# Packing four column blocks of the conditioning matrix on the 128 partitions, with their schedule moved, in a two-layer hybrid decoder

## The chip, the cores and the metric

One core of a Trainium2 chip runs the whole program in one launch. The metric is the device time in microseconds (us) of one execution, the median of several runs. The core has a matrix engine (PE, with its weight loads PEld), a vector engine (DVE), a scalar engine (ACT), a general engine (POOL) and a synchronising engine (SP) that here only issues DMAs.

## The reference

A sequence of 1024 tokens with 1024 features goes through two layers. Each layer first turns a conditioning vector c into six vectors of 1024 numbers:

```python
c_act = jax.nn.silu(c)
for l in range(DEPTH):
    mod = (c_act @ ada_w[l] + ada_b[l])[:, None, :]
    sh1, sc1, g1, sh2, sc2, g2 = jnp.split(mod, N_MOD, axis=-1)
    h = rms_norm(x, norm1_w[l]) * (1.0 + sc1) + sh1
    x = x + g1 * hybrid_mixer(h, w_in[l], w_out[l], ...)
    h = rms_norm(x, norm2_w[l]) * (1.0 + sc2) + sh2
    x = x + g2 * conv_ffn(h, w_gate[l], w_val[l], conv_w[l], conv_b[l], w_down[l])
return rms_norm(x, final_norm_w)
```

`ada_w[l]` is 1024 x 6144 in float32, 25.2 MB a layer. The mixer has four retention heads and four HGRN2 heads over one input projection, and one output projection. The MLP is gated, of width 2816, with a causal convolution of three taps on the gate. Everything is float32.

## The kernel before, in words

Activations lie with features on the partitions. Products run as three passes of split operands (high part, low part). A layer goes through these stages: the first units of the input projection; the heads (L862 to L882) and their gates (L885 to L897), whose projections are pairs of column blocks made of seven products (`pair`, L456); the output projection `wo` (L923 to L941); the first units of the gated MLP and its 20 pairs (L969 to L995); the down projection over three groups of feature tiles, 8, 8 and 6 (L1018 to L1038, and L1066 to L1075 for the last group, `dn_last`).

The conditioning work is called ada. `ada_w[l]` is cut into 12 blocks b of 512 columns; block b gives entries 4b to 4b+3 of the tile `mod` (128 features each). For one block, `ada_steps` (L159) takes eight loads of 128 rows x 512 columns into the tile `aw` (two buffers, SP's queue) and multiplies and adds each into the accumulator `ac` (one buffer) with the activated c of its rows as a per-partition factor: one DVE operation a load, at L165 for the first and L167 for the others. `ADA_WAIT` = 4 empty steps later, `ada_finish` (L147) sums the accumulator over the partitions with four float32 matmuls against a column of ones (L150, two passes each, into the PSUM tile `aps`), adds `ada_b` (L152), and for the scales makes `modA` (L156).

`ada_steps` is a generator: every call of `tick` (L177) goes one step further in the block that is being worked on, and a block takes 13 calls. Ticks stand in `step` (L384), which the units and pairs call after each product, and after each half in the first two groups of the down projection (L1034). Blocks 4 to 11 of layer 0 are put on the list in the first head (L877), the 12 blocks of layer 1 ahead of layer 0's MLP (L948), behind `ada_all` (L946), which runs what is left. Blocks 0 to 3 of layer 0 are made at the start by `ada_first` (L192) with loads of 512 KB, in the order 2, 0 (scale and shift of the first four feature tiles), then 3, 1.

The order of the instructions of an engine is set when the program is built, by a list scheduler that works with priorities: the place in the program text, less an offset under `hp()` (L59). The weight loads (`load_raw`, L333, two buffers on SP's queue), the splits of weights into two parts (`piece`, L326) and the additions of a product to the residual (`resid`, L908) have that offset; ada has not. An engine and its DMA queue then work in that order. Products use four PSUM banks (`pr`), transposes, sums and `aps` four others (`at`).

```python
def tick():
    if not ada_now and ada_todo:
        ada_now.append(ada_steps(*ada_todo.pop(0)))
    if ada_now and next(ada_now[0], True):
        ada_now.pop()
```

Of the kernel before, what the change touches and what calls it, by code (L numbers as in the profile page):

```python
# [9 lines left out]
F32 = mybir.dt.float32  # L10
# [4 lines left out]
ALU = mybir.AluOpType  # L15

P = 128
# [23 lines left out]
def kernel(  # L41
# [60 lines left out]

# [1 line left out]
    vec_c0 = [("c", c_in.rearrange("b (r p) -> (b r) p", p=P), 8)]  # L104
    vec_a = [("n1", norm1_w.rearrange("l (r p) -> (l r) p", p=P), 16),
# [27 lines left out]

    load_cols(0, vec_c0, nc.sync)

    def cl(name, i, n=1):
        t, r0 = col[name]
        return t[:, r0 + i:r0 + i + n]

    cact = const.tile([P, KT], F32, name="cact")  # L140
    A.activation(cact, cl("c", 0, 8), AF.Silu)

# [1 line left out]
    mod = const.tile([P, DEPTH * 48], F32, name="mod")  # L144
    modA = const.tile([P, DEPTH * 16], F32, name="modA")

    def ada_finish(l, b, a):  # L147
        ps = at_ps(f"aps{l}_{b}")
        for j in range(4):
            T.matmul(ps[:, j:j + 1], a[:, j * P:(j + 1) * P], onec, start=True, stop=True)  # L150
        o = l * 48 + b * 4
        V.tensor_tensor(out=mod[:, o:o + 4], in0=ps[:, 0:4], in1=cl("ab", o, 4), op=ALU.add)  # L152
        if b in (2, 3, 8, 9):
            which, i = (0, b - 2) if b < 4 else (1, b - 8)
            e = l * 16 + which * 8 + i * 4
            V.scalar_tensor_tensor(out=modA[:, e:e + 4], in0=mod[:, o:o + 4], scalar=1.0,  # L156
                                   in1=cl("n2" if which else "n1", l * 8 + i * 4, 4), op0=ALU.add, op1=ALU.mult)

    def ada_steps(l, b):  # L159
        a = stg.tile([P, HALF], F32, tag="ac", bufs=1, name=f"ac{l}_{b}")  # L160
        for k in range(KT):
            raw = stg.tile([P, HALF], F32, tag="aw", bufs=2, name=f"aw{l}_{b}_{k}")
            nc.sync.dma_start(out=raw, in_=ada_w[l, k * P:(k + 1) * P, b * HALF:(b + 1) * HALF])
            if k == 0:
                V.tensor_scalar_mul(a, raw, cact[:, 0:1])  # L165
            else:
                V.scalar_tensor_tensor(out=a, in0=raw, scalar=cact[:, k:k + 1], in1=a,  # L167
                                       op0=ALU.mult, op1=ALU.add)
            yield
        for _ in range(ADA_WAIT):  # L170
            yield
        ada_finish(l, b, a)

# [18 lines left out]
    def ada_first(b):  # L192
        acc = Z()
        a = acc.t[:, 0:HALF]
        for kp in range(4):
            raw = boot_pool.tile([P, S], F32, tag="boot", name=f"af{b}_{kp}")
            rv = raw[:, :].rearrange("p (a n) -> p a n", a=2)
            last_load[0] = nc.sync.dma_start(
                out=rv,
                in_=ada_w[0, kp * 256:(kp + 1) * 256, b * HALF:(b + 1) * HALF].rearrange("(a p) n -> p a n", p=P))  # L200
            for j in range(2):
                k = kp * 2 + j
                if k == 0:
                    V.tensor_scalar_mul(a, rv[:, 0, :], cact[:, 0:1])
                else:
                    V.scalar_tensor_tensor(out=a, in0=rv[:, j, :], scalar=cact[:, k:k + 1], in1=a,
                                           op0=ALU.mult, op1=ALU.add)
        ada_finish(0, b, a)
        acc.free()
# [4 lines left out]

# [1 line left out]

# [107 lines left out]

# [1 line left out]
    def piece(src, n, nm):  # L326
# [43 lines left out]

    chains = []

    def room(n):
# [10 lines left out]
    def step():  # L384
        tick()
        for ch in list(chains):
            ch[0] -= 1
            if ch[0] <= 0:
                ch[0] = next(ch[1], 0)
                if ch[0] == 0:  # L390
                    chains.remove(ch)
# [18 lines left out]

# [1 line left out]
    def split(dst, k, src):  # L412
# [120 lines left out]

# [1 line left out]
    def transpose8(src, nm, evac):  # L535
# [222 lines left out]

# [1 line left out]
    xs = [Z() for _ in range(KT)]  # L760
# [11 lines left out]
    first.keep()  # L772
    ada_first(2)
    ada_first(0)
# [3 lines left out]
    def start_units():  # L778
# [14 lines left out]
        spill_x(1, hi, nc.gpsimd)  # L793
        ada_first(3)
        ada_first(1)
# [50 lines left out]
    for l in range(DEPTH):  # L846
# [1 line left out]
        early = []  # L848
# [13 lines left out]
        for h in range(HEADS):  # L862
# [13 lines left out]
            if l == 0 and h == 0:  # L876
                ada_todo.extend((0, b) for b in range(4, 12))  # L877
            run(value_chain(a, box, "h", f"h{l}_{h}v"))
# [38 lines left out]
        def wo_cols(n):  # L917
            w = wcols(w_out, l, n * P, f"wo{l}_{n}")
            return [w[i] for i in order]

        xs = []
        load_xs(0, xd[2 * l])
        for n in range(5):  # L923
            load_xs(n + 1, xd[2 * l])
            w = wo_cols(n)
            for half in range(2):
                ps = pr_ps(f"wo{l}_{n}_{half}")
                slot_mm(ps, w, places, half)
                resid(ps, n, half, 16, xd[2 * l + 1])
        tail = {n: wo_cols(n) for n in range(5, KT)}  # L930
# [4 lines left out]
        for half in range(2):  # L935
            for n in range(5, KT):
                ps = pr_ps(f"wo{l}_{n}_{half}")
                slot_mm(ps, tail[n], places, half, hooks.get(n) if half else None)
                resid(ps, n, half, 16, xd[2 * l + 1])
            if half == 0:  # L940
                first.sums()  # L941
        second = TokenNorm(1, l, 1)
        second.sums()

# [1 line left out]
        ada_all()  # L946
        if l + 1 < DEPTH:
            ada_todo.extend((l + 1, b) for b in range(12))  # L948

        def conv_act(g, v, ft, order=None):  # L950
# [16 lines left out]
            tmp.free()  # L967

        parts = [(w_gate, l, 0, f"f{l}_0g"), (w_val, l, 0, f"f{l}_0v")]  # L969
        gps, vps = first_units([wcols(*p) for p in parts], [p[3] for p in parts], second)  # L970
# [25 lines left out]

# [1 line left out]
        places = (sum([slots(b) for b in (b11, tops[2], b21, tops[3])], []), sum([slots(b) for b in (b12, b22, b11, b21)], []),  # L998
# [19 lines left out]
        for gi, n in enumerate(GROUPS[:-1]):  # L1018
# [9 lines left out]
            for d in range(KT):  # L1028
                if gi == 0 and d + 1 < KT:
                    load_xs(d + 1, xd[2 * l + 1])  # L1030
                pss = [pr_ps(f"dn{l}_{gi}_{d}_{half}") for half in range(2)]
                for half in range(2):
                    slot_mm(pss[half], w, groups[gi], half)
                    tick()  # L1034
                w = dw(d + 1) if d + 1 < KT else None
                for half in range(2):
                    resid(pss[half], d, half, 40)
            fill(gi + 1, fresh[gi + 1], GROUPS[gi + 1])  # L1038
        f0 = starts[-1]
        nm = f"dn{l}_last"  # L1040
# [100 lines left out]
```

## Time and profile before

| | us |
|---|---|
| median of three runs (2641.31 to 2644.66) | 2642.14 |
| span of the profiled execution | 2637.6 |
| PE busy in it | 2519.4 |
| DVE busy | 1839.7 |
| ACT busy | 986.1 |
| POOL busy | 592.0 |

The time shown of the profiled execution is its span, from the first to the last instruction of the program; the runs are timed from outside it, and their median is 4.5 us above. PE's granted clock has a mean of 0.980. In the profile, `line engine op out<-in` names a group of instructions by its line in the kernel and its tiles with the numbers left out: `f` are the MLP's products, `dn` the down projection's first two groups, `wo` the output projection's, `g` the gates', `h`, `v` and `r` the heads', `aw`, `ac` and `aps` the tiles of ada, `af` the loads of `ada_first`.

### The profile page before, as it was taken

Reading aid. Unit: us, or ns where it says so; the run is one execution under the profiler, and the core shown is the slowest. Engines: PE = TensorE matmul, PEld = TensorE weight load, DVE = VectorE, ACT = ScalarE, POOL = GpSimd, SP = SyncE. Lnnn points to the kernel's source line nnn. Section 1 sums busy time; section 2 is a strip of 40 time slices with the busy share of each in tenths; the row PEclk is TensorE's granted clock in tenths of the full one; section 3 lists DMA queues with packets and bytes.
Section 4 is the critical chain, followed back from the end, with each engine's and each line's share of the span. In section 5 each row is a group of like instructions: output and inputs, shape, how many; then the busy total and the mean of one; then the engine's idle time right before and its main releaser. Section 6 shows DMA issues by size and latency. Waiting matters only on the chain.

```text
span 2637.6 us, 32740 instructions
## 1 busy us (share of the span) xinstructions
PE 2519.4 (96%) x12189; PEld 2072.7 (79%) x12189; DVE 1839.7 (70%) x2781; ACT 986.1 (37%) x1685; POOL 592.0 (22%) x480
## 2 busy tenths in 40 slices
PE   5889999999999999899999899999999999999998
PEld 4777877877788888788877788888877888887887
DVE  6988788765987788834377777777387677674435
ACT  4533433333533333412264334444154333342224
POOL 1512223210423323200023222222033332320000
PEclk8999999999999999999999999999999999999999
DMA  8222322552234344732231112224212222254213
GB/s 293 69 86 86 104 77 82 174 187 80 71 121 132 126 140 151 245 125 94 86 108 56 50 39 64 73 73 160 92 56 76 84 76 88 80 198 138 96 53 107
DMA packets 293920, 283.56 MB, mean 108 GB/s; under 512 B 10793, under 2 KB 240769, under 8 KB 293761
## 3 DMA queue, kind: packets, MB, share of 16 engines
q1 hardware_dynamic: 275904, 219.42, 26.7%
q0 software_dynamic: 17408, 61.88, 6.5%
q8 instruction: 96, 1.57, 0.2%
q14 instruction: 63, 0.52, 0.1%
q10 hardware_dynamic: 449, 0.17, 0.0%
HBM read 229.00 MB, written 52.43 MB: 107 GB/s over the span
## 4 chain that ended last, share of the span: by engine, by line
PE 71%; DVE 12%; issue 10%; POOL 4%; DMA 2%; ACT 2%; POOLq 0%; SPq 0%; DVEq 0%; ACTq 0%
PE f L451 6%; PE f L453 6%; PE f L452 6%; PE dn L528 4%; PE dn L526 4%; PE dn L527 4%; PE lh L712 2%; PE wo L526 2%; PE wo L528 2%; PE wo L527 2%; PE g L451 2%; PE g L452 2%; PE g L453 2%; PE dn_last L526 2%; PE dn_last L528 2%
## 5 line engine op out<-in xcount | busy, mean ns | idle before, releaser
L451 PE MATMUL f<-hhi,whif 128*128 128x512 f32 x640 | 253.8, 397 | 1.9 <-DVE z L485 1.8
L453 PE MATMUL f<-hhi,wlof 128*128 128x512 f32 x640 | 251.4, 393 | 0.0
L452 PE MATMUL f<-hlo,whif 128*128 128x512 f32 x640 | 250.1, 391 | 0.0
L485 DVE TENSOR_TENSOR z<-z,f 128x512 f32<-128x512 f32 x238 | 161.5, 682 | 63.1 <-PE f L453 54.0
L451 PE MATMUL f<-thi,whif 128*128 128x512 f32 x480 | 190.2, 396 | 6.0 <-ACT z L491 4.0
L452 PE MATMUL f<-tlo,whif 128*128 128x512 f32 x480 | 190.0, 396 | 0.0
L453 PE MATMUL f<-thi,wlof 128*128 128x512 f32 x480 | 189.7, 395 | 0.0
L528 PE MATMUL dn<-hhi,wlodn 128*128 128x512 f32 x384 | 151.8, 395 | 9.8 <-DVE wlodn L330 9.8
L526 PE MATMUL dn<-hhi,whidn 128*128 128x512 f32 x384 | 151.6, 395 | 0.0
L527 PE MATMUL dn<-hlo,whidn 128*128 128x512 f32 x384 | 150.1, 391 | 0.0
L167 DVE SCALAR_TENSOR_TENSOR ac<-aw,cact,ac 128x512 f32<-128x512 f32 x140 | 130.7, 934 | 22.8 <-DMA aw<-in_ada_w_dram 22.0
L912 DVE SCALAR_TENSOR_TENSOR z<-dn,mod,z 128x512 f32<-128x512 f32 x64 | 48.0, 750 | 136.3 <-PE dn L528 136.1
L453 PEld LDWEIGHTS f<-hhi,wlof 128*128 128x128 f32 x640 | 120.7, 189 | 28.4
L451 PEld LDWEIGHTS f<-hhi,whif 128*128 128x128 f32 x640 | 120.5, 188 | 28.3 <-DVE z L485 2.3
L452 PEld LDWEIGHTS f<-hlo,whif 128*128 128x128 f32 x640 | 120.6, 188 | 26.9
L451 PEld LDWEIGHTS f<-thi,whif 128*128 128x128 f32 x480 | 90.6, 189 | 29.7 <-ACT z L491 4.9
L915 POOL DMA_DIRECT2D xd<-z x48 | 26.0, 541 | 390.4 <-DVE z L912 362.5
L329 ACT ACTIVATE whidn<-rawdn 128x512 fp32r<-128x512 f32 x64 | 39.5, 627 | 186.1 <-PE dn L527 173.3
L453 PEld LDWEIGHTS f<-thi,wlof 128*128 128x128 f32 x480 | 90.6, 189 | 20.9
L452 PEld LDWEIGHTS f<-tlo,whif 128*128 128x128 f32 x480 | 90.2, 188 | 20.6
L712 PEld LDWEIGHTS lh<-z,z 128*128 128x128 f32 x640 | 80.1, 199 | 24.1 <-issue 19.6
L712 PE MATMUL lh<-z,z 128*128 128x64 f32 x640 | 80.1, 280 | 17.1 <-DVE z L731 16.3
(664 smaller groups left out, 6868.7 us busy)
## 6 DMA issues: line engine op xcount, KB each, us to landing
aw<-in_ada_w_dram SPq DMA_DIRECT2D x160, 256.0 KB, 2.7
acts<-z POOLq DMA_DIRECT2D x44, 512.0 KB, 3.2
z<-acts SPq DMA_DIRECT2D x44, 512.0 KB, 4.3
z<-xd POOLq DMA_DIRECT2D x32, 512.0 KB, 5.7
rawdn<-in_w_down_dram SPq DMA_DIRECT2D x32, 512.0 KB, 3.8
xd<-z POOLq DMA_DIRECT2D x52, 256.0 KB, 2.7
rawdn_last<-in_w_down_dram SPq DMA_DIRECT2D x32, 384.0 KB, 3.4
af<-in_ada_w_dram SPq DMA_DIRECT2D x16, 512.0 KB, 9.9
```

What stands on the lines that cost most here:

```text
L167: V.scalar_tensor_tensor(out=a, in0=raw, scalar=cact[:, k:k + 1], in1=a, op0=ALU.mult, op1=ALU.add)
L329: A.activation(hi[:, 0:n], src, AF.Copy)
L451: T.matmul(ps, wh, rh, start=k == 0, stop=False)
L452: T.matmul(ps, wh, rl, start=False, stop=False)
L453: T.matmul(ps, wl, rh, start=False, stop=k == 3)
L485: V.tensor_add(o, x, ps)
L526: T.matmul(ps, a, rh, start=i == 0, stop=False)
L527: T.matmul(ps, a, rl, start=False, stop=False)
L528: T.matmul(ps, b, rh, start=False, stop=i == last)
L712: T.matmul(ps[:, c * 64:(c + 1) * 64].rearrange("p (b t) -> p b t", t=s), k.t[:, cs], qp.t[:, cs].rearrange("p (b t) -> p b t", t=s)[:, 1: ...
L912: V.scalar_tensor_tensor(out=x, in0=ps, scalar=mod[:, l * 48 + gate + d:][:, 0:1], in1=x, op0=ALU.mult, op1=ALU.add)
L915: nc.gpsimd.dma_start(out=dst[d, :, sl], in_=x)
```

## The change

A load of `ada_steps` now takes 32 rows of four neighbouring blocks: block q of the four lies on partitions 32q to 32q+31. A pack of four blocks needs 32 loads of 256 KB, 32 operations and 37 steps. Its finish makes the four matmuls against a mask `msk` of four columns (column q is one on block q's partitions), so that one pass gives the sums of all four blocks. There are two packs of layer 0 (blocks 4 and 8) and three of layer 1 (0, 4 and 8). `ada_first` packs two blocks on 64 partitions each, b and b + 2, with 16 loads of 256 KB a pack, each into one half of the partitions. The factors are laid out anew by `load_c` for two and for four blocks.

The ticks change place: none in the MLP's units and pairs of either layer (`quiet`), two behind each half of the output projection's first five column tiles and of the first half of its last three, and three in place of one behind each half of the down projection. Layer 1's packs are put on the list ahead of the output projection, and `ada_all` stands ahead of it and again behind the second group of the down projection.

```diff
+    def load_c(q):
+        n = P // q
+        zz = Z()
+        src = c_in.rearrange("b (j r) -> (b j) r", r=n)
+        for i in range(q):
+            nc.sync.dma_start(out=zz.t[0:D // n, i * n:(i + 1) * n], in_=src)
+        ps = at_ps(f"cps{q}")
+        T.transpose(ps[:, 0:D // n], zz.t[0:D // n, 0:P], ident[0:D // n, 0:D // n])
+        cact[q] = const.tile([P, D // n], F32, name=f"cact{q}")
+        A.activation(cact[q], ps[:, 0:D // n], AF.Silu)
+        zz.free()
+        msk[q] = const.tile([P, q], F32, name=f"msk{q}")
+        V.memset(msk[q], 0.0)
+        for i in range(q):
+            V.memset(msk[q][i * n:(i + 1) * n, i:i + 1], 1.0)
...
-    def ada_finish(l, b, a):
+    def ada_finish(l, b, gap, q, a):
         ps = at_ps(f"aps{l}_{b}")
         for j in range(4):
-            T.matmul(ps[:, j:j + 1], a[:, j * P:(j + 1) * P], onec, start=True, stop=True)
+            T.matmul(ps[:, j * q:(j + 1) * q], a[:, j * P:(j + 1) * P], msk[q], start=True, stop=True)
...
     def ada_steps(l, b):
         a = stg.tile([P, HALF], F32, tag="ac", bufs=1, name=f"ac{l}_{b}")
-        for k in range(KT):
+        for k in range(32):
             raw = stg.tile([P, HALF], F32, tag="aw", bufs=2, name=f"aw{l}_{b}_{k}")
-            nc.sync.dma_start(out=raw, in_=ada_w[l, k * P:(k + 1) * P, b * HALF:(b + 1) * HALF])
+            nc.sync.dma_start(out=raw, in_=ada_w[l, k * 32:(k + 1) * 32, b * HALF:(b + 4) * HALF].rearrange(
+                "r (q n) -> q r n", q=4))
...
-        ada_finish(l, b, a)
+        ada_finish(l, b, 1, 4, a)
+        if b != 4:
+            ada_scale(l, b // 8, 0, 8)
...
     def ada_first(b):
...
-        for kp in range(4):
+        for kp in range(8):
             raw = boot_pool.tile([P, S], F32, tag="boot", name=f"af{b}_{kp}")
             rv = raw[:, :].rearrange("p (a n) -> p a n", a=2)
-            last_load[0] = nc.sync.dma_start(
-                out=rv,
-                in_=ada_w[0, kp * 256:(kp + 1) * 256, b * HALF:(b + 1) * HALF].rearrange("(a p) n -> p a n", p=P))
+            for q in range(2):
+                last_load[0] = nc.sync.dma_start(
+                    out=rv[q * 64:(q + 1) * 64],
+                    in_=ada_w[0, kp * 128:(kp + 1) * 128, (b + 2 * q) * HALF:(b + 2 * q + 1) * HALF].rearrange(
+                        "(a r) n -> r a n", r=64))
...
     def step():
-        tick()
+        if not quiet[0]:
+            tick()
...
-    ada_first(2)
+    load_c(4)
     ada_first(0)
...
-        ada_first(3)
         ada_first(1)
...
-                ada_todo.extend((0, b) for b in range(4, 12))
+                ada_todo.extend((0, b) for b in (4, 8))
...
+        ada_all()
+        if l + 1 < DEPTH:
+            ada_todo.extend((l + 1, b) for b in (0, 4, 8))
         xs = []
         load_xs(0, xd[2 * l])
         for n in range(5):
...
                 slot_mm(ps, w, places, half)
+                tick()
+                tick()
                 resid(ps, n, half, 16, xd[2 * l + 1])
...
+                if not half:
+                    tick()
+                    tick()
                 resid(ps, n, half, 16, xd[2 * l + 1])
...
-        ada_all()
-        if l + 1 < DEPTH:
-            ada_todo.extend((l + 1, b) for b in range(12))
...
+        quiet[0] = True
         parts = [(w_gate, l, 0, f"f{l}_0g"), (w_val, l, 0, f"f{l}_0v")]
...
                     slot_mm(pss[half], w, groups[gi], half)
                     tick()
+                    tick()
+                    tick()
...
+        quiet[0] = False
+        ada_all()
```

## Rows read from the trace of the kernel before

**Rows 1.** The page's first line of busy times, and its chain that ended last by engine.
```profile
PE 2519.4 (96%) x12189; PEld 2072.7 (79%) x12189; DVE 1839.7 (70%) x2781; ACT 986.1 (37%) x1685; POOL 592.0 (22%) x480
...
PE 71%; DVE 12%; issue 10%; POOL 4%; DMA 2%; ACT 2%; POOLq 0%; SPq 0%; DVEq 0%; ACTq 0%
```

**Rows 2.** Windows: length, busy PE, PEld, DVE, ACT, POOL (count), clock, DMA share, GB/s.
```profile
99.70:551.50 451.80, 415.82 (x2425) 350.73 (x2424) 370.48 (x620) 173.60 (x358) 116.34 (x79) 0.97 0.34 107
...
694.60:1098.90 404.30, 399.99 (x1761) 325.43 (x1760) 335.89 (x443) 145.49 (x218) 126.91 (x103) 1.00 0.45 142
1098.90:1286.00 187.10, 179.46 (x778) 146.26 (x777) 76.54 (x101) 37.31 (x50) 2.64 (x5) 0.98 0.36 117
1407.00:1836.30 429.30, 406.81 (x2361) 343.55 (x2360) 315.82 (x534) 171.79 (x351) 104.30 (x74) 0.98 0.23 73
...
1978.00:2370.30 392.30, 388.69 (x1680) 315.60 (x1679) 280.38 (x353) 149.69 (x218) 122.28 (x106) 1.00 0.30 98
2370.30:2551.40 181.10, 178.98 (x771) 145.64 (x770) 66.99 (x86) 37.51 (x51) 1.06 (x2) 0.99 0.31 102
```

**Rows 3.** Timeline of PE around one finish: start, length, instruction.
```profile
450.40 0.95 PE L150 MATMUL aps<-onec,ac 128*128 128x1 f32 x8
451.27 1.15 PE L722 MATMUL lh<-z,z 128*64 128x64 f32 x16
```

**Rows 4.** Groups by line, whole span: busy us, mean ns, idle before and releasers.
```profile
L167 DVE SCALAR_TENSOR_TENSOR ac<-aw,cact,ac 128x512 f32<-128x512 f32 x140 | 130.7, 934 | 22.8 <-DMA aw<-in_ada_w_dram 22.0
...
L150 PE MATMUL aps<-onec,ac 128*128 128x1 f32 x160 | 18.9, 239 | 0.0
```

**Rows 5.** Timeline of DVE: finishes of three blocks, one block's first operation.
```profile
287.10 0.16 DVE L152 TENSOR_TENSOR mod<-aps,cols 128x4 f32<-128x4 f32 x1
...
454.05 0.15 DVE L152 TENSOR_TENSOR mod<-aps,cols 128x4 f32<-128x4 f32 x1
...
543.22 0.15 DVE L152 TENSOR_TENSOR mod<-aps,cols 128x4 f32<-128x4 f32 x1
543.29 0.48 DVE L165 TENSOR_SCALAR ac<-aw,cact 128x512 f32<-128x512 f32 x1
```

**Rows 6.** Tile `ac` in the heads, then in two blocks: durations, first and last start.
```profile
L167 DVE SCALAR_TENSOR_TENSOR ac<-aw,cact,ac x57: 734/746/2853, 122.3 to 543.8; 128x512 f32<-128x512 f32 x57
L165 DVE TENSOR_SCALAR ac<-aw,cact x9: 475/479/485, 121.8 to 543.3; 128x512 f32<-128x512 f32 x9
...
L167 DVE SCALAR_TENSOR_TENSOR ac<-aw,cact,ac x7: 734/743/2853, 456.9 to 474.0; 128x512 f32<-128x512 f32 x7
...
L167 DVE SCALAR_TENSOR_TENSOR ac<-aw,cact,ac x7: 740/745/752, 226.4 to 251.7; 128x512 f32<-128x512 f32 x7
```

**Rows 7.** The page's DMA queues (packets, MB, share of 16 engines) and one load.
```profile
q0 software_dynamic: 17408, 61.88, 6.5%
...
q10 hardware_dynamic: 449, 0.17, 0.0%
...
aw<-in_ada_w_dram SPq DMA_DIRECT2D x160, 256.0 KB, 2.7
```

**Rows 8.** Timeline of DVE in the down projection: start, length, instruction, idle before.
```profile
1132.97 0.75 DVE L167 SCALAR_TENSOR_TENSOR ac<-aw,cact,ac 128x512 f32<-128x512 f32 x1 [0.85 <-DMA aw<-in_ada_w_dram]
...
1143.27 0.75 DVE L167 SCALAR_TENSOR_TENSOR ac<-aw,cact,ac 128x512 f32<-128x512 f32 x1 [1.31 <-DMA aw<-in_ada_w_dram]
...
1147.51 0.75 DVE L912 SCALAR_TENSOR_TENSOR z<-dn,mod,z 128x512 f32<-128x512 f32 x1 [2.22 <-PE dn L528]
...
1153.07 0.75 DVE L912 SCALAR_TENSOR_TENSOR z<-dn,mod,z 128x512 f32<-128x512 f32 x1 [1.66 <-PE dn L528]
```

**Rows 9.** Window of the start, columns as in rows 2.
```profile
12.00:24.00 12.00, 9.24 (x46) 8.49 (x44) 7.99 (x28) 7.35 (x13) 0.00 (x0) 0.88 1.07 364
```

**Rows 10.** Line L198, the loads of `ada_first`: durations of an issue, first and last start.
```profile
L198 SPq DMA_DIRECT2D af<-in_ada_w_dram x16: 368/522/799, 7.1 to 31.2; - x16
```

**Rows 11.** Timeline of PE at the start.
```profile
30.28 1.87 PE L150 MATMUL aps<-onec,z 128*128 128x1 f32 x8 [6.75 <-DVE z L206]
```

More of the change, by code (lines that the diff above doesn't have):

```diff
@@ L100, in open_tops @@
             tops[i + 1] = (thi[:, i], tlo[:, i])
-    vec_c0 = [("c", c_in.rearrange("b (r p) -> (b r) p", p=P), 8)]
     vec_a = [("n1", norm1_w.rearrange("l (r p) -> (l r) p", p=P), 16),
@@ L132, in load_cols @@
             zz.free()
-    load_cols(0, vec_c0, nc.sync)
+    msk, cact = {}, {}
+    def load_c(q):
[13 more added lines that the diff above has]
+            V.memset(msk[q][i * n:(i + 1) * n, i:i + 1], 1.0)
+    load_c(2)
     def cl(name, i, n=1):
@@ L138, in cl @@
         return t[:, r0 + i:r0 + i + n]
-    cact = const.tile([P, KT], F32, name="cact")
-    A.activation(cact, cl("c", 0, 8), AF.Silu)
     mod = const.tile([P, DEPTH * 48], F32, name="mod")
     modA = const.tile([P, DEPTH * 16], F32, name="modA")
-    def ada_finish(l, b, a):
+    def ada_finish(l, b, gap, q, a):
         ps = at_ps(f"aps{l}_{b}")
         for j in range(4):
-            T.matmul(ps[:, j:j + 1], a[:, j * P:(j + 1) * P], onec, start=True, stop=True)
+            T.matmul(ps[:, j * q:(j + 1) * q], a[:, j * P:(j + 1) * P], msk[q], start=True, stop=True)
@@ L151, in ada_finish @@
         o = l * 48 + b * 4
[L152 to L157, printed above, removed]
+        pick = lambda t: t.rearrange("p (q m) -> p q m", q=q)[:, :, 0:4]
@@ L159, in ada_steps, with ada_scale @@
+        V.tensor_tensor(out=pick(mod[:, o:o + q * gap * 4]), in0=ps[:, 0:4 * q].rearrange("p (j q) -> p q j", q=q),
+                        in1=pick(cl("ab", o, q * gap * 4)), op=ALU.add)
+    def ada_scale(l, which, i, n):
+        e, o = l * 16 + which * 8 + i, l * 48 + which * 24 + 8 + i
+        V.scalar_tensor_tensor(out=modA[:, e:e + n], in0=mod[:, o:o + n], scalar=1.0,
+                               in1=cl("n2" if which else "n1", l * 8 + i, n), op0=ALU.add, op1=ALU.mult)
     def ada_steps(l, b):
@@ L160, in ada_steps @@
         a = stg.tile([P, HALF], F32, tag="ac", bufs=1, name=f"ac{l}_{b}")
-        for k in range(KT):
+        for k in range(32):
             raw = stg.tile([P, HALF], F32, tag="aw", bufs=2, name=f"aw{l}_{b}_{k}")
-            nc.sync.dma_start(out=raw, in_=ada_w[l, k * P:(k + 1) * P, b * HALF:(b + 1) * HALF])
+            nc.sync.dma_start(out=raw, in_=ada_w[l, k * 32:(k + 1) * 32, b * HALF:(b + 4) * HALF].rearrange(
+                "r (q n) -> q r n", q=4))
             if k == 0:
-                V.tensor_scalar_mul(a, raw, cact[:, 0:1])
+                V.tensor_scalar_mul(a, raw, cact[4][:, 0:1])
@@ L166, in ada_steps @@
             else:
-                V.scalar_tensor_tensor(out=a, in0=raw, scalar=cact[:, k:k + 1], in1=a,
+                V.scalar_tensor_tensor(out=a, in0=raw, scalar=cact[4][:, k:k + 1], in1=a,
                                        op0=ALU.mult, op1=ALU.add)
@@ L203, in ada_first @@
                 if k == 0:
-                    V.tensor_scalar_mul(a, rv[:, 0, :], cact[:, 0:1])
+                    V.tensor_scalar_mul(a, rv[:, 0, :], cact[2][:, 0:1])
                 else:
-                    V.scalar_tensor_tensor(out=a, in0=rv[:, j, :], scalar=cact[:, k:k + 1], in1=a,
+                    V.scalar_tensor_tensor(out=a, in0=rv[:, j, :], scalar=cact[2][:, k:k + 1], in1=a,
                                            op0=ALU.mult, op1=ALU.add)
-        ada_finish(0, b, a)
+        ada_finish(0, b, 2, 2, a)
+        ada_scale(0, 0, b * 4, 4)
         acc.free()
@@ L371 @@
     chains = []
+    quiet = [False]
     def room(n):
```

## The prediction

> **What bounds the kernel now.** I read the page's totals and the chain of waits first. PE is busy 96% of the span and carries 71% of the chain that ended last, with DVE next at 12% [rows 1]: time is won only where PE waits or does avoidable work, and lost wherever something makes PE wait. Then I cut the span at the first matmul of each stage and laid the stages of layer 0, which carry the modulation work (ada: loads, accumulating DVE operations, summing matmuls), beside the same stages of layer 1, which carry none [rows 2]. That gives the present price of this work. The heads and gates take 451.8 us against 429.3, the pairs of the MLP 404.3 against 392.3, the first two groups of the down projection 187.1 against 181.1. So all the work that the change touches costs about 40 us after the start.
>
> The sum is made against the profiled execution: span 2637.6 us. The median of the runs, 2642.1, is 4.5 us above that span and holds what lies around it. The prediction is for the median. A difference under 0.2% (5.3 us) is what a measurement of this kernel cannot tell from none.
>
> **What is removed.** A block's finish is eight passes of PE, one after the other: 0.87 us from its start to that of the next matmul, 450.40 to 451.27 [rows 3]. With four blocks in one pass it happens 5 times in place of 20, and twice in place of 4 at the start. Three more columns in a pass, which lasts 239 ns by the mean [rows 4], I cost at nothing. The 17 small additions that go with the finishes (0.15 us of DVE each) I leave out of the sum, as a gain of at most 2.6 us. The accumulating operations do not become fewer: a pack of four blocks has 32, as four blocks of eight had, each 934 ns by the mean [rows 4], each with a 256 KB load.
>
> - The MLP's pairs lose all of this work. The diff also stops the ticks there. They become what layer 1's are: **-12**.
> - The down projection's base becomes that of layer 1: **-6** (mostly its start, where DVE was late with the last column tile).
> - The heads lose six finishes: 6 x 0.87 = **-5**.
> - Three finishes land in the down projection: 3 x 0.87 = **+3**.
>
> **Where the work really goes.** The diff writes 26 ticks into the output projection and 96 into the down projection. The rows say that a block does not wait for its tick: the first operation of layer 1's first block ran at 543.29, right behind the finish of layer 0's last block at 543.22 [rows 5]. Its written place is in the MLP's pairs, which start at 694.6. What holds a block back is only its single accumulator, which comes free at the finish before it. The finish itself stays near its written place: a block takes 13 steps, and the third and sixth block's finishes (steps 39 and 78) stand at 287.10 and 454.05 [rows 5], 4.3 us per step. So I expect: layer 0's two packs run from about 122 and from the 37th step (about 278 us), layer 1's first pack runs from the 74th step (about 437) and so still among the gates, its finish waits until the down projection, and the other two packs, 64 operations, run in the down projection, each as fast as its loads and DVE allow.
>
> - The heads and gates then hold 96 operations in place of 66, 57 and 9 [rows 6]. The 66 with their 8 finishes cost 22.5 us over layer 1; less 8 x 0.87 that is 15.5 us, or 0.23 us each. 30 more: **+7** (0 if the surplus has another cause).
>
> **The loads.** This is the part that the trace of before does not show. A load of one block has 128 rows on both sides. The new one has 128 partitions on its target side, but its source counts 4 (column blocks) first, then 32 rows. How far a load is spread can be read off one queue: q10, the vector loads on ACT's queue, shows 449 packets and 0.17 MB [rows 7]. Those loads have 16, 16, 8, 8, 8, 8, 44, 96, 66 and 66 rows of 512 B, in all 336 rows and 0.172 MB; the other 113 packets carry next to nothing. 113 is just 16+16+8+8+8+8+11+16+11+11: one closing packet for each part, the parts being the largest number up to 16 that divides the rows. So a load's leading count sets how many DMA engines share it. With a leading count of 4 on one side, the bounds are 4 engines and 16. I take 4, because the rows follow exact divisors and 4 divides both sides, while 16 does not divide the source's 4.
>
> [...]
>
> The price goes by rows: q0, with large packets, moved 61.88 MB in 6.5% of 16 engines' span, that is 44 us per MB and engine [rows 7]. A quarter of 256 KB per engine takes 2.8 us (64 KB), a sixteenth 0.7. A load that lands in 2.7 us [rows 7] would land in about 4.8. Two buffers and 0.75 us of DVE then allow one operation per (4.8 + 0.75)/2 = 2.8 us, which is also what the four engines allow when they serve nothing else.
>
> - *Down projection.* Other traffic takes a share of 0.31 of the engines there [rows 2], so 2.8 becomes up to 2.8/(1 - 0.31) = 4.1 us; as the stage stretches by a third that share falls to about 0.23, so 3.6. The spacing now is (1143.27 - 1132.97)/5 = 2.06 us [rows 8]. DVE works in order, so a pack of 32 that was laid out at 2.06 keeps the queue back by 32 x 1.54 = 49 us, and with it the residual additions and the weight splits behind. PE bears some of that: with four PSUM banks, a half of 5.56 us (two residual additions, 1147.51 and 1153.07 [rows 8]) needs the bank of three halves earlier, a slack of 16.7 us. Loss per pack 49 - 17 = 32, for two packs 64; I take **+60**, from 2 x (32 x 0.74 - 17) = 14 (engines otherwise free) to 2 x (32 x 2.0 - 17) = 94.
> - *Heads and gates.* At a share of 0.23 [rows 2] the limit is 3.6 us. Two blocks of before were spaced (474.0 - 456.9)/6 = 2.85 and (251.7 - 226.4)/6 = 4.2 us [rows 6], mean 3.5, so DVE's own load nearly covers it. From 0 to 96 x 0.75 = 72; I take **+15**, nearer the low end since the mean spacing almost fits.
> - *Start.* The stretch from 12 to 24 us moves 364 GB/s at a full share [rows 9], and the summed loads become 32 of half the partitions, with four small loads ahead on SP's queue. Eight more issues at 0.5 us [rows 10] and four small ones delay the second half of x by up to 6 us, mostly behind the 16 operations of DVE that end at 30.28 [rows 11]; the first of its two finishes (1.9 us, beside DVE's work) goes, and the first scaled tile (0.75 us) comes behind the second. The second Silu and eight fills of small masks are taken as covered by ACT's and DVE's other work here; without that cover they cost some 2 us, which the bounds hold. **+2**, from -2 to +10.
>
> [...]
>
> SP's queue also holds the weight loads: a load of ada that waits for its buffer keeps the next weights back. That is within the lag above, since both follow DVE.
>
> **Sum:** -12 - 6 - 5 + 3 + 7 + 60 + 15 + 2 = +64 us. Span about 2701, median about **2705 us**: slower by 2.4%.
>
> **Rivals.**
> - *The loads use all 16 engines.* Then both lags vanish and the start is even: -12 - 6 - 5 + 3 + 7 = -13, about 2629 us, faster. For it: nothing in the rows shows a load with unequal sides. Against it: the exact divisors of q10. It decides at the landing: under about 3.4 us (two buffers at 2.06 us per operation) the lag is gone.
> - *Narrow loads, but an order that gives way.* If the list spreads the 64 operations evenly over the 181 us, one per 2.8 us, narrow loads just fit: -11, about 2631 us. For it: the diff's own ticks are nearly as sparse. Against it: the block that ran at once [rows 5] and the spacing of 2.06.
> - *The work stays where it is written.* Then 26 operations stand in the output projection at two per half and 70 in the down projection at three per half. At 3.6 us each a half of the latter needs 10.8 in place of 5.56: 23 halves x 5.2 - 17 = 103 us; the other terms -18, about 2727 us.
>
> **How the numbers follow.** Forecast 0.53, its own range 2650 to 2765 (the bounds of its unknown costs, not all at one end). All 16 engines 0.20, the order that gives way 0.10, the written place 0.07, and 0.10 for narrow loads with a loss that just cancels the gains, on either side of zero. Faster: 0.20 + 0.09 + 0.03 = 0.32; within 0.2%: 0.05; slower: 0.63. The range must reach to the faster rivals, since together they hold 3 in 10: from 2618 to 2770.
>
> **What would show it.** The median landing of the ada loads near 4.8 us or above in place of 2.7; the packets of SP's queue fewer although the bytes are the same; 40 summing passes in place of 160; DVE's idle time on those loads well above 22 us and mostly between 1100 and 1340; the MLP's pairs at 392 us; the first two groups of the down projection near 245 us, with PE waiting for a residual addition. A landing of 2.7 us, or a down projection near 184 us, proves the forecast wrong.

## The result and the profile after

The changed kernel takes **2862.2 us** (median of four runs, 2860.6 to 2864.5) against 2643.4 for the kernel before: a ratio of 1.083, 95% interval 1.081 to 1.084. It is slower by 219 us. The prediction named the sign and the cause, but its size, +64 us, and its range, up to 2770, were far too small.

The page of the changed kernel: busy times, SP's queue, the chain by engine, and the accumulating operations (busy us, mean ns, idle before them and what ended it).

```profile
PE 2577.5 (90%) x12054; PEld 2096.2 (73%) x12054; DVE 1828.4 (64%) x2768; ACT 989.6 (35%) x1687; POOL 569.9 (20%) x480
...
q1 hardware_dynamic: 274480, 219.44, 25.8%
...
PE 63%; DMA 15%; DVE 13%; issue 6%; POOL 2%; ACT 1%; SPq 0%; DVEq 0%; POOLq 0%; ACTq 0%
...
L185 DVE SCALAR_TENSOR_TENSOR ac<-aw,cact,ac 128x512 f32<-128x512 f32 x155 | 120.7, 779 | 248.0 <-DMA aw<-in_ada_w_dram 247.8
```

Beside [rows 1] and [rows 4]: DMA goes from 2% of the chain to 15%, and DVE's idle time before the accumulating operations from 22.8 to 248.0 us. These 225 us more are about as much as the loss of 219. That the wait is its cause, and not only its companion, the experiments below have to show.

The same page of the kernel before has for SP's queue:

```profile
q1 hardware_dynamic: 275904, 219.42, 26.7%
```

The bytes are the same and the packets 1424 fewer. That is what 4 closing packets per ada load give in place of 16: 160 x 12 = 1920 fewer, less 256 for the 16 more loads at the start and 240 for the loads of c.

Windows of the changed kernel by stage, cut at the first matmul of each; columns as in [rows 2]. In order: layer 0's heads and gates, output projection up to the MLP, MLP's pairs, first two groups of the down projection; then layer 1's heads and MLP.

```profile
104.60:666.20 561.60, 442.53 (x2377) 366.71 (x2376) 386.57 (x640) 169.24 (x352) 111.33 (x78) 0.89 0.33 97
666.20:824.30 158.10, 147.10 (x620) 116.71 (x619) 93.54 (x142) 61.64 (x97) 29.07 (x31) 0.95 0.29 89
824.30:1270.20 445.90, 409.65 (x1682) 327.72 (x1681) 298.52 (x386) 147.01 (x217) 116.94 (x106) 0.95 0.33 105
1270.20:1503.60 233.40, 191.14 (x785) 152.84 (x784) 89.48 (x121) 37.16 (x51) 1.06 (x2) 0.90 0.36 113
1624.60:2056.70 432.10, 410.19 (x2360) 345.46 (x2359) 315.91 (x534) 171.65 (x352) 104.90 (x74) 0.97 0.23 73
2197.90:2594.00 396.10, 392.49 (x1681) 315.19 (x1680) 280.67 (x352) 150.59 (x218) 119.43 (x106) 1.00 0.30 97
```

Against [rows 2] the heads and gates grew by 110 us, the stretch up to the MLP by 15, the MLP by 42, the down projection by 46, the start by 5; layer 1 hardly moved (432.1 and 396.1 us against 429.3 and 392.3). In the heads PE's busy time itself grew from 415.8 to 442.5 us with fewer instructions: the mean granted clock fell from 0.97 to 0.89 while PE waited more. So some 27 of those 110 us are matmuls run slower, not more of them.

Timeline of PE in the changed kernel, the third and the last pack's finish:

```profile
785.68 0.95 PE L165 MATMUL aps<-msk,ac 128*128 128x4 f32 x8
787.45 0.79 PE L390 MATMUL uf_0g<-hhi,whif_0g 128*128 128x512 f32 x1 [0.82 <-ACT hhi L345]
...
1459.59 0.40 PE L553 MATMUL dn<-hhi,wlodn 128*128 128x512 f32 x1
1482.32 1.87 PE L165 MATMUL aps<-msk,ac 128*128 128x4 f32 x8 [22.33 <-DVE ac L185]
```

Timeline of DVE in the changed kernel: the third pack's addition, the next pack's first operation, then two operations in the down projection.

```profile
835.18 0.16 DVE L168 TENSOR_TENSOR mod<-aps,cols 128x16 f32<-128x16 f32 x1
...
835.94 0.48 DVE L183 TENSOR_SCALAR ac<-aw,cact 128x512 f32<-128x512 f32 x1
...
1415.93 0.75 DVE L185 SCALAR_TENSOR_TENSOR ac<-aw,cact,ac 128x512 f32<-128x512 f32 x1 [2.40 <-DMA aw<-in_ada_w_dram]
1418.58 0.75 DVE L185 SCALAR_TENSOR_TENSOR ac<-aw,cact,ac 128x512 f32<-128x512 f32 x1 [1.90 <-DMA aw<-in_ada_w_dram]
```

The packs began at 127.3, 322.7, 514.3, 835.9 and 1372.0 us. The third finish stands in PE's order at 785.68, among the first products of the MLP and just ahead of a wait for ACT (787.45), so the fourth pack ran in the MLP, where the diff stops the ticks. Only the fifth ran in the down projection. There PE stood for 22.33 us in front of the last finish, whose data were late, with the projection's matmuls queued behind it.

### The profile page after: what moved, and what is told of

Read it like the earlier page. It is cut to its first block, busy times and chain, and to the rows that moved or that the text cites. A ratio compares the mean times of both kernels' runs of the same rounds, so it can differ in the third digit from the quotient of the medians.

```text
span 2861.7 us, 32494 instructions
## 1 busy us (share of the span) xinstructions
PE 2577.5 (90%) x12054; PEld 2096.2 (73%) x12054; DVE 1828.4 (64%) x2768; ACT 989.6 (35%) x1687; POOL 569.9 (20%) x480
## 4 chain that ended last, share of the span: by engine, by line
PE 63%; DMA 15%; DVE 13%; issue 6%; POOL 2%; ACT 1%; SPq 0%; DVEq 0%; POOLq 0%; ACTq 0%
DMA aw<-in_ada_w_dram 12%; PE f L476 7%; PE f L478 7%; PE f L477 7%; PE dn L553 3%; PE dn L551 3%; PE dn L552 3%; PE lh L737 2%; PE wo L551 2%; PE wo L553 2%; PE wo L552 2%; DVE ac L185 2%; PE dn_last L551 2%; PE dn_last L553 2%; PE dn_last L552 2%
## 5 line engine op out<-in xcount | busy, mean ns | idle before, releaser
L185 DVE SCALAR_TENSOR_TENSOR ac<-aw,cact,ac 128x512 f32<-128x512 f32 x155 | 120.7, 779 | 248.0 <-DMA aw<-in_ada_w_dram 247.8
```

The costliest lines, as they stand in the source:

```text
L185: V.scalar_tensor_tensor(out=a, in0=raw, scalar=cact[4][:, k:k + 1], in1=a, op0=ALU.mult, op1=ALU.add)
```

## The experiments

Theory N: the packed load's source counts 4 first, so 4 of 16 engines carry it, and DVE, which works in order, waits for it. Rival S: the place of the work costs the time.

**Wide loads in the changed kernel** (e1_wide). Rows first, then column blocks; mask and c to match.

```diff
-                "r (q n) -> q r n", q=4))
+                "r (q n) -> r q n", q=4))
```

> The changed kernel with one thing altered: its packed loads go row by row (32 rows first, then the 4 column blocks), so that partition 4r+q holds row r of block q; the cact columns and the summing mask are laid out to match. Bytes, number of loads, operations and the order on PE, ACT and DVE after the start stay. Theory N (a load whose leading count is 4 is carried by 4 of the 16 DMA engines, and DVE's queue waits for it): the loss goes, and what the packing saves stays. 2642 less 15 finishes x 0.87 plus about 5 at the start: about 2635 us, 2615 to 2650. DVE idle on the ada loads falls from 248 us to under 40; packets of SP's queue 274480 + 160 x 12 - 3 x 48 = 276256; the heads and gates of layer 0 near 450 us, the MLP's pairs near 400. Rival S (the place of the 160 operations costs the time: a pack in the MLP's pairs, one in the down projection, one accumulator): stays above 2800 us whatever carries the loads. Rival L (what counts is that a row of 2 KB comes from four far places): also above 2800.

Measured 2684.1 us, ratio 1.015 (1.013 to 1.016). SP's packets and the idle time, from its page:

```profile
q1 hardware_dynamic: 276256, 219.43, 27.5%
...
L193 DVE SCALAR_TENSOR_TENSOR ac<-aw,cact,ac 128x512 f32<-128x512 f32 x155 | 129.9, 838 | 55.5 <-DMA aw<-in_ada_w_dram 54.2
```

Windows of the heads, the MLP and the down projection:

```profile
104.80:570.80 466.00, 420.09 (x2378) 351.82 (x2377) 390.00 (x641) 171.72 (x355) 112.85 (x78) 0.95 0.38 118
...
720.10:1128.00 407.90, 395.78 (x1682) 316.20 (x1680) 302.63 (x386) 147.12 (x217) 120.33 (x106) 1.00 0.36 115
1128.00:1316.90 188.90, 184.29 (x786) 148.37 (x785) 89.30 (x121) 37.54 (x51) 1.07 (x2) 0.98 0.45 139
```

The packets are the number expected, and **178 of the 219 us go with the order of one access pattern**: by the profiles 95.6 in the heads, 38.0 in the MLP, 44.5 in the down projection, and 9 between. (These add up to 187: the profiled run of e1_wide was the fastest of its four, 2675.7 us against 2683.0 to 2685.3.) With 96, 32 and 32 operations that is 1.0, 1.2 and 1.4 us for each. S falls, and so does L, the rival that rows from four far places cost the time. But 39 us remain where the expectation had none.

**Narrow loads in the kernel before** (e2_narrow4, e2_narrow8). Only its loads are altered, and the columns of c.

```diff
-            nc.sync.dma_start(out=raw, in_=ada_w[l, k * P:(k + 1) * P, b * HALF:(b + 1) * HALF])
+            nc.sync.dma_start(out=raw, in_=ada_w[l, k * P:(k + 1) * P, b * HALF:(b + 1) * HALF].rearrange(
+                "(r q) n -> q r n", q=NQ))
```

With NQ = 4:

> The kernel before with only its 160 ada loads altered: the same 128 rows of 2 KB, taken as 4 groups of 32 (every fourth row), so that the source counts 4 first; the cact columns follow. Blocks, finishes, ticks and the order of PE and DVE stay those of before. Theory N: the loss of the change appears without the change: the changed kernel loses about 50 us per 32 operations (heads, MLP and down projection alike), so 160 lose about 220: 2860 us, 2780 to 2920; DVE idle on the ada loads from 22 us to 200 or more; packets of SP's queue 275904 - 160 x 12 + 24 = 274008. Rival S: 2642, within 10 us.

Measured 2806.5 us, ratio 1.062 (1.060 to 1.063). From its page, then windows of the heads and the MLP:

```profile
q1 hardware_dynamic: 274000, 219.42, 26.4%
...
L178 DVE SCALAR_TENSOR_TENSOR ac<-aw,cactn,ac 128x512 f32<-128x512 f32 x140 | 119.2, 851 | 199.1 <-DMA aw<-in_ada_w_dram 198.6
```

```profile
99.40:611.60 512.20, 435.09 (x2426) 363.98 (x2426) 364.21 (x619) 172.83 (x356) 112.37 (x79) 0.93 0.32 94
...
755.20:1256.20 501.00, 434.37 (x1761) 339.83 (x1760) 329.63 (x443) 144.07 (x217) 118.70 (x104) 0.94 0.39 115
```

The loss appears without the change: 161 us, 60 in the heads for 66 operations and 97 in the MLP for 88. The packets are 4 closing ones per load (the 8 under the expected count are a slip in the sum: the extra load of c has 8 rows and 8 closing packets).

With NQ = 8:

> e2_narrow4 with 8 groups of 16 rows in place of 4 of 32: the source counts 8 first. Theory N: 8 engines carry a load, 32 KB each, so one operation per 1.4 us is the floor and few spacings of the kernel before are under it: 2645 to 2680 us, DVE idle on the ada loads 30 to 80 us, packets of SP's queue 275904 - 160 x 8 + 16 = 274640. Rival R (any load whose rows are taken out of order or in groups costs the same): near 2806, as with 4 groups.

Measured 2704.7 us, ratio 1.023 (1.021 to 1.024), so 60 us more than before, beyond the expected 35. From its page:

```profile
q1 hardware_dynamic: 274640, 219.42, 27.0%
...
L178 DVE SCALAR_TENSOR_TENSOR ac<-aw,cactn,ac 128x512 f32<-128x512 f32 x140 | 124.7, 891 | 94.3 <-DMA aw<-in_ada_w_dram 93.7
```

The loss runs with the leading count: 0 with 16 closing packets a load, 60 us with 8, 161 us with 4. Rival R, that any load taken in groups costs the same, falls.

**The start of before, with wide loads** (e5_wide_oldstart). Four blocks of 128 rows each; shown is what selects them.

```diff
-    load_c(2)
+    load_c(1)
...
-        ada_finish(0, b, 2, 2, a)
+        ada_finish(0, b, 1, 1, a)
```

> e1_wide with the start of before: four blocks of 128 rows by four loads each, four finishes, in place of two packs of two by loads of 64 partitions. If the half-width loads at the start cost what the stage cut shows (r starts at 104.6 in place of 99.7 us), this is 3 to 7 us faster than e1_wide; if the start is even, within 3 us of it.

Measured 2667.5 us, ratio 1.0090 (1.0075 to 1.0105): 16.6 us faster than with the packed start by the medians, while by the profiles the window of the heads begins at 96.8 in place of 104.8, 8.0 us sooner. The pair e4_wide_oldplace and e7_wide_unpaced below differs in the start too, and there the medians are 8.7 us apart. Windows of the start, first of the changed kernel (12 to 24 us, where SP's queue moves almost only half-width loads), then of this one (12 to 18 us, where it moves only the full-width ones):

```profile
12.00:18.00 6.00, 5.26 (x30) 4.90 (x31) 3.10 (x18) 5.84 (x11) 0.00 (x0) 1.00 0.89 217
18.00:24.00 6.00, 0.88 (x9) 0.72 (x7) 5.62 (x16) 2.85 (x5) 0.00 (x0) 0.57 1.07 245
```

```profile
12.00:18.00 6.00, 3.69 (x24) 2.52 (x22) 5.54 (x21) 5.50 (x11) 0.00 (x0) 1.00 1.04 379
```

At a full DMA share (last column but one, 1.07 and 1.04) the half-width loads move 245 GB/s, the full-width ones 379.

**The place of the work** (e4_wide_oldplace, e7_wide_unpaced). Wide loads with the ticks where they were before, first with the packed start, then with the old one; the ticks between the matmuls of the output and down projections go too.

```diff
-        ada_all()
-        if l + 1 < DEPTH:
-            ada_todo.extend((l + 1, b) for b in (0, 4, 8))
         xs = []
...
-        quiet[0] = True
+        ada_all()
+        if l + 1 < DEPTH:
+            ada_todo.extend((l + 1, b) for b in (0, 4, 8))
```

> e1_wide with the ticks put back where the kernel before has them (every step of heads, gates and MLP; none added in the output and down projections), so packing without the move. Theory N: the place matters little once loads are wide; within 15 us of e1_wide, 2620 to 2650. Rival S: at least 100 us faster than e1_wide.

> Packs of four blocks with wide loads, the start of before and the ticks where the kernel before has them: e5_wide_oldstart and e4_wide_oldplace in one. 2667 less the 5 us between e1 and e4: about 2662, 2652 to 2672.

Measured 2678.7 us (ratio 1.013, 1.011 to 1.015) and 2670.0 us (1.009, 1.008 to 1.011): within 6 us of the same kernels with the moved ticks. With wide loads, moving the ticks is worth next to nothing either way. It moves little, too: only the fifth pack changes its stage, and begins at 938 in place of 1231 us in one pair and at 923 in place of 1222 in the other. What the move is worth with narrow loads no run shows.

**Pace** (e6_wide_paced, e9_wide_spread). In the kernel of e7_wide_unpaced, each accumulating operation is put behind the last addition of its own step on DVE's queue; the second kernel adds an idle step after every second operation and waits 2 steps in place of 4 ahead of the finish.

```diff
-            with nullcontext():
+            with paced():
                 if k == 0:
...
             yield
+            if k % 2:
+                yield
```

> e7_wide_unpaced with each accumulating operation of the packs put behind the last addition of its own step in DVE's queue, so that a pack spreads over its 37 steps. Theory D (what is left of the loss with wide loads, some 22 us without the start, comes of a pack's 32 operations running as densely as DVE allows once the accumulator is free): 20 to 30 us faster than e7, near 2635. Rival: the operations cost DVE the same wherever they stand, within 6 us of e7.

> e6_wide_paced with one idle step after every second operation and a shorter wait before the finish (51 steps a pack in place of 37), so that the 160 operations fill the steps of heads, gates and MLP evenly: 64 in the heads and gates over some 106 steps. Theory D (density decides): the heads cost per operation what they cost before, 0.22 us in place of 0.44 in e6; heads and gates near 447 us in place of 461, the MLP near 400, in all 2630 to 2640, faster than the kernel before by 0.2 to 0.5%. Rival: pacing has nothing left to give, 2647 as e6.

Measured 2647.3 us (ratio 1.0012, 1.0003 to 1.0022) and 2642.0 us (0.9991, 0.9982 to 1.0001). Windows of the heads and the MLP, unpaced, paced, spread:

```profile
95.40:561.40 466.00, 420.68 (x2378) 351.24 (x2377) 396.92 (x643) 173.41 (x357) 113.75 (x80) 0.96 0.39 119
710.30:1124.40 414.10, 399.52 (x1698) 317.37 (x1697) 328.16 (x421) 145.58 (x217) 126.15 (x106) 1.00 0.42 132
```

```profile
97.00:558.00 461.00, 419.01 (x2378) 349.70 (x2378) 369.94 (x616) 176.75 (x359) 115.21 (x80) 0.96 0.34 104
699.40:1100.60 401.20, 397.20 (x1705) 319.37 (x1704) 351.11 (x448) 144.65 (x217) 130.59 (x106) 1.00 0.49 154
```

```profile
97.00:551.80 454.80, 415.46 (x2377) 348.24 (x2376) 373.49 (x617) 176.66 (x359) 119.08 (x80) 0.96 0.34 106
693.20:1091.30 398.10, 394.49 (x1697) 317.56 (x1696) 333.02 (x439) 147.02 (x217) 127.98 (x106) 1.00 0.49 152
```

Pacing is worth 22.8 us. The MLP shows it best: 414 to 401 us, although it then holds 91 of the 160 accumulating operations in place of 64. A pack that may run as soon as its accumulator is free crowds DVE there, where PE needs it. In the heads the gain is not shown: 466 to 461 us, with 64 operations in place of 96. Another 7.5 us lie between the two stages (148.9 to 141.4), which hold none of these operations unpaced and 5 paced; their cause stays open. Spreading further gives 5 more and brings the heads to 454.8 with the same 64 operations, not the 447 expected. The spread kernel is level with the kernel before; it does not beat it.

**Pace with narrow loads** (e8_narrow_paced), the second rival of the prediction: the paced kernel with the loads of the changed one.

> e6_wide_paced with the loads of the changed kernel (4 column blocks first). The order that gives way, second rival of the prediction: with operations some 4.3 us apart a narrow load of 2.7 us fits between, and it is within 30 us of e6. Otherwise, if other traffic on the same 4 engines or the pairs of loads keep DVE waiting at that spacing too, it is 80 us or more slower than e6.

Measured 2770.5 us, ratio 1.048 (1.046 to 1.049). From its page:

```profile
L192 DVE SCALAR_TENSOR_TENSOR ac<-aw,cact,ac 128x512 f32<-128x512 f32 x155 | 127.7, 824 | 134.6 <-DMA aw<-in_ada_w_dram 134.1
```

It is 123 us slower than e6, and DVE's idle time on the ada loads is 134.1 us against 7.5. An order that gives way softens the narrow loads but does not make them fit.

**Which engines, and how many loads at once** (e10_two_queues, e11_pool_queue, e12_three_buffers). The changed kernel with its odd loads on ACT's queue; with all on POOL's; with three buffers.

```diff
-            nc.sync.dma_start(out=raw, in_=ada_w[l, k * 32:(k + 1) * 32, ...
+            (nc.scalar if k % 2 else nc.sync).dma_start(out=raw, in_=ada_w[l, k * 32:(k + 1) * 32, ...
```

> The changed kernel with its odd ada loads issued from ACT's queue in place of SP's. If every load whose source counts 4 is carried by the same 4 engines, two queues share them and the floor between operations in the down projection stays at 2.65 to 2.7 us; 2862, within 40 us. If one queue carries one such load after the other and a second queue brings other engines, the floor falls to about 1.35 us, and DVE idle on the ada loads from 248 to under 130 us; 2720 to 2790.

Measured 2854.9 us (ratio 1.080, 1.078 to 1.082), idle on the loads 241.0 us. From its page:

```profile
q10 hardware_dynamic: 11009, 21.15, 2.3%
...
L185 DVE SCALAR_TENSOR_TENSOR ac<-aw,cact,ac 128x512 f32<-128x512 f32 x155 | 120.9, 780 | 241.2 <-DMA aw<-in_ada_w_dram 241.0
```

ACT's queue went from 449 to 11009 packets: 80 x (128 + 4). That the time stays does not yet show that both queues share the same 4 engines, since two buffers would hold back a faster pair of queues too. The trace shows it. A window of the last pack, in which only ada loads move, on both queues (columns as before, DMA share and GB/s last):

```profile
1401.00:1406.00 5.00, 3.96 (x18) 2.87 (x16) 1.64 (x3) 0.00 (x0) 0.00 (x0) 1.00 0.25 84
```

The share stays at 4 of 16 engines. At 254 moments of the last pack, sampled every 0.05 us, packets of both queues were in flight, and 203 times they were 4 together, never more than 6.

> The changed kernel with all its packed ada loads issued from POOL's queue in place of SP's. Two queues shared the same 4 engines in e10. If POOL's queue gives each load 4 engines in turn, two loads in flight do not share engines: the floor between operations in the down projection falls from 2.65 towards 1.4 us, DVE idle on the ada loads from 248 to 60 to 150 us, 2690 to 2800 in all. If the engines are the same whatever the queue, 2862 within 40 us; if POOL's own work holds the issues back, slower than 2862 and DVE idle above 248 us.

Measured 2863.0 us (ratio 1.083, 1.080 to 1.086). From its page:

```profile
aw<-in_ada_w_dram POOLq DMA_DIRECT2D x160, 256.0 KB, 5.9
```

This is the one place where a narrow load's landing is shown: 5.9 us against 2.7 [rows 7]. The time is what was expected if the engines are the same whatever the queue, but for another reason: with two buffers, a landing of 5.9 us and 0.75 us of DVE give one operation per 3.3 us even if the engines differ. The trace shows that here they do differ at times. A window of the last pack with two loads in flight and no other transfer:

```profile
1448.00:1449.50 1.50, 1.50 (x8) 1.21 (x7) 0.00 (x0) 0.00 (x0) 0.00 (x0) 1.00 0.51 157
```

Half of the 16 engines' time is taken, and 157 GB/s are moved, where two queues of the run before kept to 0.25 and 84. On POOL's queue a load also comes to 272 packets in place of 132, so its count can't be read beside that of SP's.

> The changed kernel with three buffers for the ada loads in place of two (and, to make room, five in place of six for the low halves of the weights). If two buffers and a landing near 5.9 us set the mean of 3.53 us between operations of the last pack, a third brings it to the floor of the 4 engines, 2.65 to 2.9 us, DVE idle on the ada loads from 248 to 120 to 180 us and the time to 2740 to 2810. If the 4 engines are the limit at all times, 2862 within 20 us. If the fifth buffer of the weights matters more than either, slower.

Measured 2854.0 us (ratio 1.081, 1.079 to 1.083). Timeline of DVE in its down projection; a window of its last pack in which only ada loads move; ACT's waits for weights between 1264 and 1500 us; and the order of SP's queue beside one of those waits:

```profile
1295.63 0.75 DVE L185 SCALAR_TENSOR_TENSOR ac<-aw,cact,ac 128x512 f32<-128x512 f32 x1 [1.26 <-DMA aw<-in_ada_w_dram]
1298.31 0.75 DVE L185 SCALAR_TENSOR_TENSOR ac<-aw,cact,ac 128x512 f32<-128x512 f32 x1 [1.92 <-DMA aw<-in_ada_w_dram]
```

```profile
1406.50:1420.00 13.50, 5.98 (x18) 4.47 (x17) 4.06 (x6) 1.15 (x2) 0.00 (x0) 0.75 0.26 98
```

```profile
ACT whidn L352 <- DMA rawdn<-in_w_down_dram: 158.8, 7, 25.2
```

```profile
1302.36 0.45 SPq L363 DMA_DIRECT2D rawdn<-in_w_down_dram  x1
1304.44 24.26 SPq L180 DMA_DIRECT2D aw<-in_ada_w_dram  x9
1328.77 0.45 SPq L363 DMA_DIRECT2D rawdn<-in_w_down_dram  x1
...
1337.90 1.15 ACT L352 ACTIVATE whidn<-rawdn 128x512 fp32r<-128x512 f32 x2 [25.23 <-DMA rawdn<-in_w_down_dram]
```

A third buffer does bring the operations of these packs to the floor, 2.68 us apart for long stretches, and with three loads on their way the engines still move 98 GB/s at a share of 0.26: four of 16. It gains only 8 us by the medians (0.2% by the ratios, whose intervals overlap), and DVE's idle time on the ada loads stays at 233.8 us, well above the expectation. The third finish kept its place here, so the MLP without a pack took 394.3 us and the down projection with two 257.0; the heads took 578.1. The weights of the down projection now wait: ACT stood 158.8 us for them, against 34.7 in the changed kernel between 1270 and 1504, which had one pack there. SP's lines show why: nine ada loads stand between two weight loads on its queue, so the weight loads were issued 26.4 us apart, and ACT's wait of 25.23 us is that interval less its own 1.15. The weight load itself took 9.1 us from its issue to ACT's use, against a median landing of 3.8 in the kernel before, so it came later as well, but the 26.4 us between the issues are the larger part. (One buffer fewer for the low halves of the weights is in this run as well.)

## Why the prediction was wrong in size

**What closes the sum.** By medians: 2862.2, less 178.1 for wide loads, 16.6 for the start, 22.8 for the pace, plus 2.5 for the place, gives 2647.2; the kernel before stood at 2639 to 2646 in these comparisons. The terms follow one path through the runs (after, e1, e5, e7, e6), so they add up by construction; what they show is that nothing is left at its end. By the other way round the start is 8.7 and the place -5.4, so each small term is good to some 8 us.

**Term by term**, forecast against the profiles: heads and gates -5 + 7 + 15 = +17, measured +110; the stretch up to the MLP no term, +15; the MLP -12, +42; the down projection -6 + 3 + 60 = +57, +46; the start +2, +5; the rest none, +6. In all +64 against +224.

- **Four engines: right.** The share of 0.26 with loads always on their way (e12) and of 0.25 with two queues at work (e10) shows it, and the floor of 2.65 us (estimated 2.8) and the loss by leading count (161 us with 4, 60 with 8) go with it. The closing packets go with the source's count although the target has 128 partitions: 4 per load where the source counts 4 (e2_narrow4), 8 where it counts 8 (e2_narrow8).
- **The step that failed: heads and gates, +15, "nearer the low end since the mean spacing almost fits".** Measured: 95.6 us by e1_wide, above even the bound of 72. A mean spacing of 3.25 to 3.5 against a limit of 3.6 says nothing, since operations come in bursts. Of the 57 spacings inside blocks of the heads in the kernel before, 33 are under 3.6 us, and what they lack adds up to 64.6 us; the narrow loads cost the kernel before 60.4 us in that stage (e2_narrow4). Over all 140 spacings the same sum gives 173 us, against 161 measured. The sum leans on its limit: with 2.65 us in place of 3.6 it gives 36 and 91. Time spent in a long spacing is not paid back to a short one, because DVE works in order. The trace for this sum was at hand; I averaged it.
- **MLP, -12: wrong, +42.** The step that failed is "its finish waits until the down projection". It stands in PE's order at 785.68, which freed the accumulator some 500 us ahead of its written place, the 11th of the 96 ticks of a stage that began at 1270.2. The rule that I took from [rows 5], that a block starts when the accumulator is free, held four times out of four, within 4 us; I did not apply the same freedom to the finish.
- **Down projection, +57: measured +46, but for one pack, not two.** A pack cost 46 us where I had 30. Twenty-two of them are PE waiting at the finish, a wait that I had not seen: the finish's matmuls stand in PE's order in front of the projection's. In the run with three buffers both packs landed there, and the stage took 257.0 us against the 245 forecast. So +57 came near +46 by luck: too many packs at too low a price.
- **30 more operations in the heads, +7 less 5: too small.** With wide loads that stage still grew by 14 us. The 0.23 us were read from blocks that pause for 5 steps after every 8, and a pack does not pause. That this is the reason is not shown: spreading the same 64 operations (e6 to e9) took 6 us off the heads, but pacing, which took 32 of 96 operations out of them, only 5.
- **The stretch up to the MLP, no term: measured +15.** With wide loads it grew by 6, so 9 of the 15 go with the narrow loads.
- **Start, +2, bounds -2 to +10: the stage began 4.9 us later than before and 8.0 later than in the same kernel with the old start; by medians 16.6 (e1 to e5), beyond the bound, or 8.7 (e4 to e7), inside it.** About 8 of the 16.6 are the distance of the profiled run of e1 from its median, so they are not in its profile, and where they lie stays open. The price was near the upper bound, and I took a value near the lower one. Both bounds were my estimates: the trace of before holds no half-width load of ada. In the changed kernel such loads moved 245 GB/s (18 to 24 us), in e5 the full-width ones 379 (12 to 18 us), both at a full DMA share; why they move less is not shown.
- **The saved finishes (15 fewer at 0.87 us, -13 over layer 0): not seen in the total.** The spread kernel has 40 summing passes in place of 160, wide loads and the old start, and is level with the kernel before. In the MLP, with eight finishes fewer and 84 operations in place of 80, it took 398.1 us against 404.3; its heads took 454.8 against 451.8, with 64 operations in place of 66. What lengthens the heads was not settled.
- **The rivals.** All 16 engines: refuted by the packets (4 closing ones a load) and the share (0.25 in e10, 0.26 in e12). The order that gives way: with operations paced to their own steps, further apart than this rival asked for, narrow loads still cost 123 us. The work where it is written: not what happened, though 2727 was the nearest of my figures.
- **Two slips in the working, neither of weight:** [rows 2] give the DMA share of layer 1's down projection as 0.32, not 0.31, and 2 x (32 x 0.74 - 17) is 13.4, not 14.

## What to carry to other kernels

Before packing several column blocks into one load, write out which count comes first in its source: here one transposed access pattern cost 178 us with the same bytes, loads and operations. Price a slower producer of an in-order engine by the sum over the single spacings that fall short, not by the mean; here that sum, worked out afterwards, came within 8% of what was measured. Where a tile framework lets work run as soon as a buffer is free, ask what each finish, and not only each start, may slip into.

## What was not expected of the hardware

On SP's queue an ada load had 16, 8 or 4 closing packets (before, e2_narrow8, e2_narrow4), on ACT's 4 (e10), and with 4 the engines' share was 0.25 (e10) and 0.26 (e12) of 16: here one number of the page told how far a load was spread. For 8 the share was not read. Two queues of loads with a leading count of 4 shared the same four engines (0.25 of 16 with both at work), while two such loads from POOL's queue took 0.51 at times. And at three buffers the operations ran at the floor of 2.68 us while the total moved by only 8 us: the weight loads, nine ada loads apart on SP's queue, now set the pace.
